# A hybrid attention block on one core: differences of a level in one GpSimd step, norms' halves in tiles of their own, and regrouped matmuls in the output projection

## The chip, the core and the metric

The kernel runs on one core of a Trainium2 chip. A core has TensorE (PE in the profile, with its weight loads as PEld), VectorE (DVE), ScalarE (ACT), GpSimd (POOL) and SyncE (SP, which here only issues DMAs). Each works through its own instructions in a fixed order and waits at semaphores for the others. The metric is the time of one execution on the device in microseconds (us).

## What is computed

One layer of a diffusion backbone, with 256 latent and 256 context tokens of width 2048, all in float32. Its core, cut to what the change touches:

```python
def gla_scan(q, k, v, log_a, s0):            # gated linear attention, 8 heads, forward and backward
    def step(state, inp):
        qc, kc, vc, ac = inp
        b = jnp.cumsum(ac, axis=2)
        o_inter = jnp.einsum('bhid,bhde->bhie', qc * jnp.exp(b), state)
        rel = b[:, :, :, None, :] - b[:, :, None, :, :]
        decay = jnp.exp(jnp.where(lower, rel, -jnp.inf))
        scores = jnp.einsum('bhid,bhjd,bhijd->bhij', qc, kc, decay)
        ...

def hybrid_layer(...):
    h_l = modulate(rms_norm(x, norm1_w), sh1, sc1)
    ... = jnp.split(h_l @ w_in, IN_OFFSETS, axis=-1)        # the same for the context tokens
    ...                                                    # GLA heads: gla_scan both ways
    q_l = rope_2d(diff_qk(dq_l, diff_qnorm_w), ang_row, ang_col)   # rms_norm of each half head
    k_l = rope_2d(diff_qk(dk_l, diff_knorm_w), ang_row, ang_col)
    ...                                                    # differential attention: 8 heads
    g_a, g_b = jnp.split(jax.nn.sigmoid(h @ w_gate + b_gate), 2, axis=-1)
    mix_l = (g_a * (ya @ w_proj_gla) + g_b * (yb @ w_proj_diff)) @ w_out
    x_new = x + g1 * mix_l
    ...                                                    # second norm, conv_ffn, residual
```

## The kernel before

**Precision and weights.** A float32 matrix product is made of products of halves: `split` (L207) copies a weight tile on ACT into `whi` (L212) and subtracts on DVE into `wlo` (L219); both lie in rings of three buffers (tags `hi` and `lo`), each 128x1024. `split_act` (L236) does the same with activations into tiles that its caller gives (L237 on ACT, L238 on DVE). `col_tile` (L255) then makes, for each of 16 weight blocks, one matmul over 512 columns with `whi` (L281, "h") and one over 256 with `wlo` (L283, "l"). `col_tile2` makes three of 512 columns per block (L356 to L358), `value_rows` three of 272 or 512 (L294 to L296).

**Order of the h and l matmuls.** In every run of four blocks the order is `TURN` (h0 l0 h1 l1 h2 l2 h3 l3), or, where `orders` (L249) says so, `SHIFTED` (h0 h1 l0 h2 l1 h3 l2 l3) in two of every seven runs. The output projection, tile `mix`, has 16 output tiles c; it asks for `orders(c, KT // 4, 1, 5)`, so c = 1 to 5 have such runs and c = 6 to 15 have `TURN` alone.

**Stages.** After a first norm and a sweep over the first weights (to about 125 us) come the GLA stage, with the values (`gvb`), queries and keys (`gq`, `gk`), the keys of the other attention (`dk`) and the output gates (`gr`) as matmuls that keep PE busy; then the differential attention (`dvb`, `dq`, the scores `s`) among the `gate` tiles; the two projections (`pga`, `pgb`), `mix`, and the feed-forward part (`upg`, `upv`, `down`), which the change leaves alone.

**A pair of GLA heads.** `gla_pair` (L799) runs four times, with priority over the matmuls around it. Two matmuls (`z`, L812) give the log decays of both directions; four ACT steps each (L816 to L819) and one DVE step (L820) make `m`; DVE scans (L824 to L833) make the cumulative sums `bfb` (forward in row 0, backward in row 1). The scores within 128 tokens are then made at seven levels of halving, m = 64 to 1. For one level `factors` (L899) takes four differences on GpSimd into `e` (L916 to L919: queries and keys, first and second half of every block, each 128x128), one exponential on ACT (L920) and one product with q and k on DVE (L921). `e` has a ring of four buffers. `scored` (L871) runs the score matmuls `sc` (L882) of a group of levels and puts them into `at`: two copies per head on ACT (L932, L933), masked copies on DVE (L929). Groups are: two products that need no level, with levels 0 and 1; levels 2 to 4; levels 5 and 6. Between the first two groups PE transposes the keys (`kT`, L857), which ACT copies to `kn` (L858).

**Norms of the attention's queries and keys.** `heads_norm` (L659) copies a finished `dk` or `dq` tile out of its bank on ACT, squares it into `nsq`, splits the squares with `split`, so through the rings of the weights, sums them with two matmuls (`hss`, L656 and L657), and finishes with ACT and DVE (L318 to L332).

**What sets the order.** No list is written out by hand for this part. The scheduler of the Tile layer orders each engine's instructions with its own estimates of durations and priorities, so an edit in one place moves instructions in others.

**VectorE's side job.** Between these steps DVE runs dot products `araw` over 128x1024 (L380) for the modulation vectors.

Of the kernel before, what the change touches and what calls it, by code (L numbers as in the profile page):

```python
# [9 lines left out]
F32 = mybir.dt.float32  # L10
# [142 lines left out]
def layer_kernel(tc, I, out):  # L153
# [3 lines left out]
    with es:  # L157
# [5 lines left out]
        def acc_bank(name):  # L163
            return ps.tile([P, 512], F32, tag="acc", bufs=4, name=name)
# [481 lines left out]
        gr = [p2.tile([P, 2 * T + 4], F32, tag=f"gr{p}", name=f"gr{p}")[:, :2 * T] for p in range(NPAIR)]  # L646
        dk = [p2.tile([P, 2 * T + 4], F32, tag=f"dk{h}", name=f"dk{h}")[:, :2 * T] for h in range(HEADS)]

        def norm_tiles():
            return [tp.tile([P, 512], F32, tag=t, name=t) for t in ("nraw", "nsq", "hny")]  # L650

        def sums(o, m, sq, halves):

# [2 lines left out]
            i = PE.matmul(o, m, lo[:, :n], start=True, stop=False)  # L656
            after(PE.matmul(o, m, hi[:, :n], start=False, stop=True), i)  # L657

        def heads_norm(b, wname, done, o, sq, y):  # L659
# [24 lines left out]
        def onormed(pool, dst, ob, w, halves=None, copy=V.tensor_copy, places=None):  # L684


            raw, sq, y = places or [pool.tile([P, T], F32, tag=t, name=t) for t in ("oraw", "osq", "ony")]
            S.activation(sq, ob[:, :T], AF.Square)
            copy(raw, ob[:, :T])
            s = aux_bank("oss")  # L690
            if halves is None:
                PE.matmul(s[:, :T], ones.bitcast(F32), sq, start=True, stop=True)
            else:
                split_act(*halves, sq)
                sums(s[:, :T], ones, sq, halves)
            rsqrt_parts(y, sq, s[:, :T], DV)
            normed_by(dst, raw, w, y, sq, DV)

        SHUF = [(j + 16) % 32 for j in range(32)]

# [36 lines left out]
        with tc.tile_pool(name="gla", bufs=1) as pg:  # L737
# [60 lines left out]

            def gla_pair(p):  # L799
                q, kl, kc = qk[p][:, 0, :], qk[p][:, 1, :], qk[p][:, 2, :]  # L800
                bfb = pg.tile([P, 2, T], F32, tag="bfb", name="bfb")
                rc = pg.tile([P, 2, T], F32, tag="rc", name="rc")
                raw = st.tile([P, 1024], F32, tag="raw", bufs=4, name="wr")
                wr = raw[:96, :2 * P].rearrange("p (a b) -> p a b", a=2)
# [93 lines left out]

                def factors(li):  # L899

                    e = pg.tile([P, 2, T], F32, tag="e", bufs=4, name="e")
                    if li is None:
                        S.activation(e[:, 0, P:], bfb[:, 0, P:], AF.Exp, scale=1.0 / 16)
                        S.activation(e[:, 0, :P], bfb[:, 1, :P], AF.Exp, scale=1.0 / 16)
                        S.activation(e[:, 1, :P], bfb[:, 0, :P], AF.Exp, scale=-1.0 / 16, bias=bl[:, 0:1])
                        S.activation(e[:, 1, P:], bfb[:, 1, P:], AF.Exp, scale=-1.0 / 16, bias=bl[:, 1:2])
                    else:
                        m = LEVELS[li]
                        g = T // (2 * m)
                        f4 = bfb[:, 0, :].rearrange("p (g h m) -> p g h m", h=2, m=m)  # L910
                        b4 = bfb[:, 1, :].rearrange("p (g h m) -> p g h m", h=2, m=m)
                        q4 = e[:, 0, :].rearrange("p (g h m) -> p g h m", h=2, m=m)
                        k4 = e[:, 1, :].rearrange("p (g h m) -> p g h m", h=2, m=m)
                        fm = f4[:, :, 0, m - 1:m].to_broadcast([P, g, m])
                        bm = b4[:, :, 1, 0:1].to_broadcast([P, g, m])
                        G.tensor_tensor(q4[:, :, 1, :], f4[:, :, 1, :], fm, op=ALU.subtract)  # L916
                        G.tensor_tensor(q4[:, :, 0, :], b4[:, :, 0, :], bm, op=ALU.subtract)
                        G.tensor_tensor(k4[:, :, 0, :], fm, f4[:, :, 0, :], op=ALU.subtract)
                        G.tensor_tensor(k4[:, :, 1, :], bm, b4[:, :, 1, :], op=ALU.subtract)  # L919
                        S.activation(e, e, AF.Exp, scale=1.0 / 16)  # L920
                    V.tensor_tensor(e, e, qk[p][:, 0:2, :], op=ALU.mult)  # L921
                    return e

# [10 lines left out]
                for n, levels in enumerate(RUNS):  # L934
                    group = ([] if n else whole) + [level(li) for li in levels]
                    if n == 1:
                        sb = scored(group[::-1], states)
                        kept = pg.tile([P, 2, T], F32, tag="e", bufs=4, name="e")
                        state = kept[:, 0, :].rearrange("p (a b) -> p a b", a=2)
                        S.copy(kept[:, 0, :], sb)  # L940
                    else:
                        scored(group[::-1])
                    if n == 0:
                        kn = turned_keys()

                obs = [aux_bank("o", j) for j in range(2)]
                for j in range(2):
# [5 lines left out]
                        PE.matmul(obs[j][:, :T], gv[:, c, h * DV:(h + 1) * DV], at[:, j, c, :],  # L953
                                  start=False, stop=c == 1)
                    if not j:
                        e = pg.tile([P, 2, T], F32, tag="e", bufs=4, name="e")
# [63 lines left out]
        with tc.tile_pool(name="diff", bufs=1) as pd:  # L1020
# [36 lines left out]
            def dq_tile(h):  # L1057
                ada_next(0.5)
                dq[h] = pd.tile([P, T], F32, tag="dq", bufs=4, name="dq")
                b = aux_bank("dq") if h < 2 else acc_bank("dq")  # L1060
                col_tile(I["w_in"][15 - NGK + h], A, b)
                heads_norm(b, nwt[:, 1:2], lambda o: roped(pd, dq[h], o, 1),
                           *[t[:, h % 2 * T:(h % 2 + 1) * T] for t in nts])

            qs, ks = {}, {}

# [34 lines left out]
            def attend(h, c):  # L1101
# [15 lines left out]
                o = pd.tile([P, T], F32, tag="ob", name="ob")  # L1117
                osq = pd.tile([P, 2, T], F32R, tag="osqs", name="osqs")
                onormed(pd, o, ob, nwt[:, 3:4], [osq[:, j, :] for j in range(2)])
# [13 lines left out]
                V.tensor_tensor(gates[j], b[:, T:], gates[j], op=ALU.add)  # L1133

            nts = norm_tiles()
            dv_chunk(0)
            for h in range(4):
                dq_tile(h)
# [298 lines left out]
```

## Time and profile before

| what | value |
|---|---|
| median of three runs | 1673.39 us (1673.18 to 1675.27) |
| the profiled execution: its own time | 1674.66 us |
| its span, first to last instruction | 1672.9 us |
| DVE busy | 1276.8 us, 76% |
| ACT busy | 898.9 us, 54% |
| granted TensorE clock, mean | 0.999 |

The span is 1.8 us shorter than the execution's own time. A row of the profile's groups gives line, engine, operation, tiles (written <- read), shape, count, then busy time and mean duration in ns, then the engine's idle time before these instructions with what ended it. A row of a timeline gives start, duration, engine and the same names, with the idle time before it in square brackets.

### The profile page before, as it was taken

Reading aid. Unit: us, or ns where it says so; the run is one execution under the profiler, and the core shown is the slowest. Engines: PE = TensorE matmul, PEld = TensorE weight load, DVE = VectorE, ACT = ScalarE, POOL = GpSimd, SP = SyncE. Lnnn points to the kernel's source line nnn. Section 1 sums busy time; section 2 is a strip of 40 time slices with the busy share of each in tenths; the row PEclk is TensorE's granted clock in tenths of the full one; section 3 lists DMA queues with packets and bytes.
Section 4 is the critical chain, followed back from the end, with each engine's and each line's share of the span. In section 5 each row is a group of like instructions: output and inputs, shape, how many; then the busy total and the mean of one; then the engine's idle time right before and its main releaser. Section 6 shows DMA issues by size and latency. Waiting matters only on the chain.

```text
span 1672.9 us, 25641 instructions
## 1 busy us (share of the span) xinstructions
PE 1655.4 (99%) x9476; PEld 1408.7 (84%) x9476; DVE 1276.8 (76%) x2013; ACT 898.9 (54%) x1475; POOL 338.0 (20%) x412
## 2 busy tenths in 40 slices
PE   9999999999999999999999999999999999999998
PEld 6679888788878888888888998888888888888887
DVE  5887877768677888788888796888888888744544
ACT  5234455654356776556655575555555555433332
POOL 0011332415011000001214101221222122584000
PEclk9999999999999999999999999999999999999999
DMA  9996735336565555797877566777777776676664
GB/s 383 408 363 216 231 129 167 114 115 207 195 222 179 189 187 194 229 288 261 275 269 233 177 204 211 237 230 229 239 240 238 220 237 214 208 221 208 219 191 137
DMA packets 111965, 372.74 MB, mean 223 GB/s; under 512 B 14560, under 2 KB 19680, under 8 KB 111840
## 3 DMA queue, kind: packets, MB, share of 16 engines
q1 hardware_dynamic: 102112, 362.51, 66.1%
q0 software_dynamic: 5696, 4.24, 1.0%
q10 hardware_dynamic: 4032, 4.37, 0.8%
q8 instruction: 74, 1.21, 0.3%
q14 instruction: 51, 0.42, 0.1%
HBM read 364.73 MB, written 2.10 MB: 219 GB/s over the span
## 4 chain that ended last, share of the span: by engine, by line
PE 91%; DVE 3%; DMA 2%; ACT 1%; POOL 1%; issue 1%; DVEq 0%; SPq 0%; ACTq 0%
PE down L1388 14%; PE upg L281 9%; PE upv L281 9%; PE gate L281 7%; PE upv L283 5%; PE upg L283 5%; PE sweep L392 4%; PE gate L283 4%; PE mix L281 4%; PE mix L283 2%; PE dvb L294 2%; PE pga L281 2%; PE pgb L281 2%; PE dvb L296 2%; PE dvb L295 2%; PE dq L281 1%
## 5 line engine op out<-in xcount | busy, mean ns | idle before, releaser
L212 ACT CAST whi<-wraw 128x1024 fp32r<-128x1024 f32 (+3 forms) x502 | 515.0, 1028 | 427.3 <-PE down L1388 138.6
L219 DVE TENSOR_TENSOR wlo<-wraw,whi 128x1024 fp32r<-128x1024 f32 (+3 forms) x466 | 562.1, 1207 | 208.4 <-ACT whi L212 203.8
L281 PE MATMUL upg<-x,whi 128*128 128x512 f32 x656 | 229.0, 391 | 0.0
L281 PE MATMUL upv<-x,whi 128*128 128x512 f32 x656 | 229.0, 391 | 0.0
L1388 PE MATMUL down<-whi,g 128*128 128x512 f32 x704 | 216.6, 389 | 0.0
L283 PE MATMUL upv<-x,wlo 128*128 128x256 f32 x656 | 182.8, 280 | 0.0
L283 PE MATMUL upg<-x,wlo 128*128 128x256 f32 x656 | 182.6, 280 | 0.0
L281 PE MATMUL gate<-x,whi 128*128 128x512 f32 x512 | 179.2, 397 | 0.0
L380 DVE CUSTOM_DVE_ANT_0 araw<-araw,cb 128x1024 f32<-128x1024 f32 x128 | 161.2, 1263 | 15.1 <-DMA araw<-in_w_ada 15.1
L219 POOL TENSOR_TENSOR wlo<-wraw,whi 128x1024 fp32r<-128x1024 f32 x36 | 87.0, 2416 | 395.4 <-ACT whi L212 395.4
L1388 PEld LDWEIGHTS down<-whi,g 128*128 128x128 f32 x704 | 132.1, 188 | 27.4
L281 PEld LDWEIGHTS upv<-x,whi 128*128 128x128 f32 x656 | 122.4, 187 | 26.6
L281 PEld LDWEIGHTS upg<-x,whi 128*128 128x128 f32 x656 | 122.4, 187 | 26.6
L283 PE MATMUL gate<-x,wlo 128*128 128x256 f32 x512 | 140.7, 284 | 0.2 <-DVE wlo L219 0.2
L1388 PE MATMUL down<-wlo,g 128*128 128x512 f32 x352 | 136.9, 389 | 0.0
L1306 DVE SCALAR_TENSOR_TENSOR C<-C,vec 128x255 f32<-128x255 f32 x88 | 105.7, 1203 | 36.6 <-ACT C L1305 36.6
L283 PEld LDWEIGHTS upg<-x,wlo 128*128 128x128 f32 x656 | 123.9, 189 | 0.5
L283 PEld LDWEIGHTS upv<-x,wlo 128*128 128x128 f32 x656 | 123.9, 189 | 0.5
L281 PEld LDWEIGHTS gate<-x,whi 128*128 128x128 f32 x512 | 94.3, 188 | 19.8 <-issue 0.7
L283 PEld LDWEIGHTS gate<-x,wlo 128*128 128x128 f32 x512 | 96.3, 189 | 5.4 <-issue 2.6
L281 PE MATMUL mix<-x,whi 128*128 128x512 f32 x256 | 88.9, 395 | 0.0
L1388 PEld LDWEIGHTS down<-wlo,g 128*128 128x128 f32 x352 | 66.1, 188 | 13.7
(332 smaller groups left out, 3235.9 us busy)
## 6 DMA issues: line engine op xcount, KB each, us to landing
wraw<-in_w_up SPq DMA_DIRECT2D x164, 512.0 KB, 4.6
araw<-in_w_ada SPq DMA_DIRECT2D x128, 512.0 KB, 5.5
wraw<-in_w_down SPq DMA_DIRECT2D x88, 512.0 KB, 4.4
wraw<-in_w_gate SPq DMA_DIRECT2D x64, 512.0 KB, 4.6
wraw<-in_w_in SPq DMA_DIRECT2D x58, 512.0 KB, 4.8
ada<-in_w_ad SPq DMA_DIRECT2D x52, 512.0 KB, 9.9
wraw<-in_w_proj SPq DMA_DIRECT2D x32, 512.0 KB, 4.9
wraw<-in_w_out SPq DMA_DIRECT2D x32, 512.0 KB, 4.7
```

What stands on the lines that cost most here:

```text
L212: copied[0] = S.copy(hi[:, :n], raw)
L219: i = e.tensor_tensor(lo[:, :n], raw, hi[:, :n].bitcast(F32), op=ALU.subtract)
L281: i = PE.matmul(b.rearrange("p (a b) -> p a b", a=2), whi[:, sl], acts[k], start=first, stop=last)
L283: i = PE.matmul(b[:, T:], wlo[:, sl], acts[k][:, 1, :], start=False, stop=last)
L294: PE.matmul(o, hi[k][:, ts], whi[:, sl], start=first, stop=False)
L295: PE.matmul(o, lo[k][:, ts], whi[:, sl], start=False, stop=False)
L296: return PE.matmul(o, hi[k][:, ts], wlo[:, sl], start=False, stop=last)
L380: i = V.tensor_tensor_reduce(raw, raw, cb[:, q * 1024:(q + 1) * 1024], 1.0, 0.0, op0=ALU.mult, op1=ALU.add, accum_out=ada2[:, j, q:q + 1])
L392: return kept(PE.matmul(*args, **kw))
L1306: V.scalar_tensor_tensor(u[:, 1:], b[:, :T - 1], vcol("conv_w", ct), u[:, 1:], op0=ALU.mult, op1=ALU.add)
L1388: i = PE.matmul(banks[h][t][n], g[:, a, ts], w[n][b], start=k == 0 and (a, b) == (1, 0), stop=k == FT - 1 and b == 1)
```

## The change

Three things are edited.

1. **Differences of a level.** GpSimd makes one subtraction per level, 128x512, into a new tile `away`: all of `bfb` minus the value at the middle of each block (for the backward row one place further, which a row length of T + 1 in the view `shifted` gives). ACT then takes two exponentials of 256 columns: with scale +1/16 for the queries and -1/16 for the keys, each reading the half blocks of the two rows crosswise. `away` has the tag `m`, one buffer, that `m` of the decays has too. The ring of `e` goes from four buffers to three.
2. **Norms.** `heads_norm` splits its squares with `split_act` into a tile `nlo` (and, for 512 columns, into a second that shares the buffer of `hny`), and takes its result tile later. In `onormed` the result may stay in `oraw`, and the shuffled tile `rt` of the queries comes from the other pool.
3. **Output projection.** `orders(c, KT // 4, 1, 14)`: two of seven runs in c = 1 to 14 are `SHIFTED`.

```diff
@@ norms
         def norm_tiles():
-            return [tp.tile([P, 512], F32, tag=t, name=t) for t in ("nraw", "nsq", "hny")]
+            return [tp.tile([P, 512], F32, tag=t, name=t) for t in ("nraw", "nsq")] + [lambda: tp.tile([P, 512], F32, tag="hny", name="hny")]
...
             def parts():
-                halves = split(sq, n)
+                low = tp.tile([P, 512], F32R, tag="nlo", name="nlo")
+                halves = [low[:, j * T:(j + 1) * T] for j in range(2)]
+                if n > T:
+                    halves = tp.tile([P, 512], F32R, tag="hny", name="nhi"), low
+                split_act(*halves, sq)

                 def rest():
+                    y = new()
                     s = acc_bank("hss")
...
@@ gla_pair
-                bfb = pg.tile([P, 2, T], F32, tag="bfb", name="bfb")
+                flat = pg.tile([P, 2 * T + 2], F32, tag="bfb", name="bfb")
+                bfb = flat[:, :2 * T].rearrange("p (a b) -> p a b", a=2)
+                shifted = flat.rearrange("p (a b) -> p a b", a=2)
...
-                    e = pg.tile([P, 2, T], F32, tag="e", bufs=4, name="e")
+                    e = pg.tile([P, 2, T], F32, tag="e", bufs=3, name="e")
...
-                        G.tensor_tensor(q4[:, :, 1, :], f4[:, :, 1, :], fm, op=ALU.subtract)
-                        G.tensor_tensor(q4[:, :, 0, :], b4[:, :, 0, :], bm, op=ALU.subtract)
-                        G.tensor_tensor(k4[:, :, 0, :], fm, f4[:, :, 0, :], op=ALU.subtract)
-                        G.tensor_tensor(k4[:, :, 1, :], bm, b4[:, :, 1, :], op=ALU.subtract)
-                        S.activation(e, e, AF.Exp, scale=1.0 / 16)
+                        away = pg.tile([P, 512], F32, tag="m", name="away")
+                        mids = shifted[:, :, m - 1:T:2 * m].unsqueeze(3).to_broadcast([P, 2, g, 2 * m])
+                        G.tensor_tensor(away.rearrange("p (a g n) -> p a g n", a=2, g=g),
+                                        bfb.rearrange("p a (g n) -> p a g n", g=g), mids, op=ALU.subtract)
+                        for i, (first, step, o, back, sign) in enumerate(((m, T - m, m, -m, 1), (0, T + m, 0, m, -1))):
+                            S.activation(view(e[:, i, :], o, [back, 2], [2 * m, g], [1, m]),
+                                         view(away, first, [step, 2], [2 * m, g], [1, m]), AF.Exp, scale=sign / 16)
...
@@ output projection
-            col_tile(I["w_out"][c], A, b, orders(c, KT // 4, 1, 5) if c else None)
+            col_tile(I["w_out"][c], A, b, orders(c, KT // 4, 1, 14) if c else None)
```

The number of matmuls stays the same; GpSimd has 84 instructions fewer, ACT 28 more. From the output projection on, all orders are as before but for the `mix` matmuls; ahead of it the scheduler has placed much anew. Three places matter below.

ACT where the first `dq` tile is finished (norm of the queries), before:

```order
L212 CAST whi<-wraw 128x1024
L290 COPY nraw<-dq 128x256
L665 ACTIVATE nsq<-nraw 128x256
L212 CAST whi<-nsq 128x256
L212 CAST whi<-wraw 128x1024 x2
L318 ACTIVATE hny<-hss,epsb 128x256
```

The same place in the change:

```order
L212 CAST whi<-wraw 128x1024
L290 COPY nraw<-dq 128x256
L212 CAST whi<-wraw 128x1024
L669 ACTIVATE nsq<-nraw 128x256
L237 CAST nlo<-nsq 128x256
L212 CAST whi<-wraw 128x1024
```

A cast of weights now stands ahead of the squares, and the cast of the squares no longer takes a buffer of the weights' ring.

DVE in the first pair of GLA heads, from the query's scaling to the products of the first levels (`rc` and `qe` are the decayed keys and queries), before:

```order
L763 SCALAR_TENSOR_TENSOR qk<-gq,qk 128x256
L219 TENSOR_TENSOR wlo<-wraw,whi 128x544
L380 ISA araw,ada_77<-araw,cb 128x1024
L380 ISA ada_77 128x1
L837 TENSOR_TENSOR rc<-rc,qk 128x512
L846 TENSOR_TENSOR qe<-qe,qk 128x512
L921 TENSOR_TENSOR e<-e,qk 128x512 x4
```

The same place in the change:

```order
L774 SCALAR_TENSOR_TENSOR qk<-gq,qk 128x256
L219 TENSOR_TENSOR wlo<-wraw,whi 128x544
L380 ISA araw,ada_77<-araw,cb 128x1024
L380 ISA ada_77 128x1
L850 TENSOR_TENSOR rc<-rc,qk 128x512
L859 TENSOR_TENSOR qe<-qe,qk 128x512
L930 TENSOR_TENSOR e<-e,qk 128x512 x2
L219 TENSOR_TENSOR wlo<-wraw,whi 128x544
L380 ISA araw,ada_77<-araw,cb 128x1024
L380 ISA ada_77 128x1
L930 TENSOR_TENSOR e<-e,qk 128x512
```

The third product, the last that the first group of scores needs, now stands behind a weight split and a dot product. On PE, in the same pair, 16 more `gvb` matmuls stand ahead of these scores.

ACT between the decays of the first pair (`z`) and the bank that the next query tile needs (`gvb`), before:

```order
L816 ACTIVATE m<-z,nba 128x512
L817 ACTIVATE l<-z,vec 128x512
L818 ACTIVATE l<-l 128x512
L819 ACTIVATE l<-l 128x512
L212 CAST whi<-wraw 128x1024
L749 COPY gv<-gvb 128x272
```

The same place in the change:

```order
L829 ACTIVATE m<-z,nba 128x512
L830 ACTIVATE l<-z,vec 128x512
L212 CAST whi<-wraw 128x1024
L831 ACTIVATE l<-l 128x512
L832 ACTIVATE l<-l 128x512
L212 CAST whi<-wraw 128x1024
L760 COPY gv<-gvb 128x272
```

Before, the first of the two 128x1024 casts stood ahead of these six rows; it now stands behind the two steps that read `z`.

More of the change, by code (lines that the diff above doesn't have):

```diff
@@ L657, in sums, with heads_norm @@
             after(PE.matmul(o, m, hi[:, :n], start=False, stop=True), i)
-        def heads_norm(b, wname, done, o, sq, y):
+        def heads_norm(b, wname, done, o, sq, new):
             n = o.shape[1]
@@ L937, in gla_pair @@
                         sb = scored(group[::-1], states)
-                        kept = pg.tile([P, 2, T], F32, tag="e", bufs=4, name="e")
+                        kept = pg.tile([P, 2, T], F32, tag="e", bufs=3, name="e")
                         state = kept[:, 0, :].rearrange("p (a b) -> p a b", a=2)
@@ L955, in gla_pair @@
                     if not j:
-                        e = pg.tile([P, 2, T], F32, tag="e", bufs=4, name="e")
+                        e = pg.tile([P, 2, T], F32, tag="e", bufs=3, name="e")
                     places = e[:, 0, :], e[:, 1, :], kept[:, 1, :]
@@ L1061, in dq_tile @@
                 col_tile(I["w_in"][15 - NGK + h], A, b)
[L1062 to L1063 removed]
+                heads_norm(b, nwt[:, 1:2], lambda o: roped(tp, dq[h], o),
+                           *[t[:, h % 2 * T:(h % 2 + 1) * T] for t in nts[:2]], lambda: nts[2][:, h % 2 * T:(h % 2 + 1) * T])
             qs, ks = {}, {}
@@ L1116, in attend @@
                     PE.matmul(ob[:, :T], dv[:, t, h * DV:(h + 1) * DV], pTs[h][:, t, :], start=t == 0, stop=t == 3)
-                o = pd.tile([P, T], F32, tag="ob", name="ob")
                 osq = pd.tile([P, 2, T], F32R, tag="osqs", name="osqs")
-                onormed(pd, o, ob, nwt[:, 3:4], [osq[:, j, :] for j in range(2)])
+                o = onormed(pd, None, ob, nwt[:, 3:4], [osq[:, j, :] for j in range(2)])
                 yb[h] = p2.tile([P, 2 * T + 4], F32R, tag=f"dk{h}", name=f"yb{h}")[:, :2 * T]
@@ L1135, in layer_kernel @@
             nts = norm_tiles()
+            nts[2] = nts[2]()
             dv_chunk(0)
```

11 lines of the change are left out of this document (5 added, 6 removed).

## The prediction

> **What bounds the kernel now.** I read the page first (busy shares), then PE's waits, then the busy time in stretches, and last the timelines around the waits.
>
> ```profile
> span 1672.9 us, 25641 instructions
> PE 1655.4 (99%) x9476; PEld 1408.7 (84%) x9476; DVE 1276.8 (76%) x2013; ACT 898.9 (54%) x1475; POOL 338.0 (20%) x412
> ```
>
> TensorE works for 99% of the span. A change that leaves its matmuls alone can win only where PE stands idle, or where its matmuls follow each other a little closer. GpSimd is busy for a fifth of the time, so 84 fewer instructions there are worth nothing by themselves. What they are worth is read from PE's waits:
>
> ```profile
> PE sc L882 <- DVE e L921: 1.9, 2, 1.6
> PE gr L281 <- ACT whi L212: 1.3, 1, 1.3
> PE gq L281 <- ACT gv L749: 1.0, 1, 1.0
> PE dq L281 <- ACT whi L212: 1.0, 2, 0.6
> PE kT L857 <- ACT at L933: 1.0, 1, 1.0
> PE dvb L294 <- ACT whi L212: 0.8, 1, 0.8
> PE sc L882 <- ACT kn L858: 0.7, 1, 0.7
> PE gr L283 <- DVE wlo L219: 0.5, 1, 0.5
> PE hss L656 <- DVE wlo L219: 0.2, 1, 0.2
> ```
>
> Columns are the total in us, the number of waits, the longest. All nine rows lie in the GLA stage and the start of the next one, and they add up to 8.4 us. That is the whole prize, 0.5% of the time; what is left of PE's idle time lies at the very start and end of the program, which the change doesn't touch. In the GLA stage idle is not the rule either:
>
> ```profile
> 160.00:200.00 40.00, 37.59 (x316) 35.55 (x314) 35.77 (x64) 22.52 (x46) 20.69 (x28) 1.00 0.67 204
> 1600.00:1640.00 40.00, 40.00 (x178) 33.14 (x177) 18.06 (x15) 15.75 (x15) 0.00 (x0) 1.00 0.63 192
> 156.00:161.90 5.90, 5.90 (x48) 5.74 (x46) 2.61 (x4) 3.66 (x6) 0.00 (x0) 1.00 0.88 315
> ```
>
> These are stretches of the span with busy time and count of PE, PEld, DVE, ACT and POOL. In the first, the first pair of heads, PE lacks 2.4 us while DVE is busy for 35.8 of 40: DVE is the crowded engine beside PE. The second gives the pace of 512-column matmuls, 40/178 = 0.225 us, the third that of the `gvb` matmuls, 5.90/48 = 0.123 us.
>
> **The change part by part. GpSimd's step.**
>
> ```profile
> L917 POOL TENSOR_TENSOR e<-bfb 128x128 f32<-128x128 f32 x28 | 22.3, 796 | 6.0 <-DVE bfb L831 6.0
> L918 POOL TENSOR_TENSOR e<-bfb 128x128 f32<-128x128 f32 x28 | 21.6, 772 | 0.0
> L916 POOL TENSOR_TENSOR e<-bfb 128x128 f32<-128x128 f32 x28 | 20.7, 739 | 117.3 <-DVE bfb L824 99.2 <-PE sc L882 12.2 <-DVE ada L380 4.4
> L919 POOL TENSOR_TENSOR e<-bfb 128x128 f32<-128x128 f32 x28 | 19.0, 677 | 0.0
> 251.15 1.41 POOL L917 TENSOR_TENSOR e<-bfb 128x128 f32<-128x128 f32 x1
> 252.52 0.40 POOL L918 TENSOR_TENSOR e<-bfb 128x128 f32<-128x128 f32 x1
> 143.82 0.74 POOL L705 TENSOR_TENSOR dk<-nraw,rope 128x256 f32<-128x256 f32 x1 [16.96 <-DVE nraw L332]
> 1205.22 2.42 POOL L219 TENSOR_TENSOR wlo<-wraw,whi 128x1024 fp32r<-128x1024 f32 x1 [8.69 <-ACT whi L212]
> ```
>
> Four steps of a level take 0.80 + 0.77 + 0.74 + 0.68 = 2.98 us on average. Undisturbed, one takes 0.40; some take 1.41. One step of 128x512 is not in the trace. Between the rows of 256 (0.74) and 1024 elements (2.42) it comes to 0.74 + 256 x 1.68/768 = 1.3 us; the two rows are its bounds, and I take 1.3 alone and up to 2.3 when it is held up once, by the 1.0 us between 1.41 and 0.40. ACT pays for it:
>
> ```profile
> L920 ACT ACTIVATE e<-e 128x512 f32<-128x512 f32 x28 | 17.6, 631 | 27.3 <-POOL e L919 27.2
> L321 ACT ACTIVATE e<-e 128x256 f32<-128x256 f32 x7 | 3.0, 425 | 0.1
> ```
>
> Two steps of 256 cost 0.85 in place of 0.63, 28 times 0.22, so 6 us more on an engine that is half idle: hidden, except where a cast for PE stands behind. On the level's own path it is 1.3 to 2.3 plus 0.85, so 2.2 to 3.2 us, against 3.0 + 0.6. But before, GpSimd began the next level while ACT worked on this one, so a level came every 3.0 us. Now `away` has one buffer, and GpSimd waits for ACT's second exponential. A level comes every 2.2 to 3.2 us, and behind a weight cast later still. **The chain of levels becomes hardly faster**; what changes is where its waits fall in PE's order. The smaller ring of `e` adds nothing within a group of three levels; across groups ACT, no longer GpSimd, waits for the score matmuls.
>
> **First pair of heads.**
>
> ```profile
> 184.27 0.44 PE L857 MATMUL kT<-ident,rc 128*128 128x128 f32 x2 [1.00 <-ACT at L933]
> 175.86 2.69 DVE L921 TENSOR_TENSOR e<-e,qk 128x512 f32<-128x512 f32 x4
> 178.47 0.71 DVE L219 TENSOR_TENSOR wlo<-wraw,whi 128x544 fp32r<-128x544 f32 x1
> L380 DVE CUSTOM_DVE_ANT_0 araw<-araw,cb 128x1024 f32<-128x1024 f32 x128 | 161.2, 1263 | 15.1 <-DMA araw<-in_w_ada 15.1
> ```
>
> Of the waits listed, 1.3 us lie here: 1.00 for `kT`, and the 0.3 by which the two waits of `sc` for `e` exceed their longest, which is the third pair's. Now the third product stands behind one more split (0.71) and one more dot product (1.26): 2.0 us later. PE has 16 more `gvb` matmuls ahead of it: 16 x 0.123 = 2.0 us. That evens out; the decays are ready about 1.2 us earlier (below), and GpSimd's longer steps hold DVE up once or twice by up to 1.3 us. In the second group `kT` still waits for copies on ACT that now stand behind both exponentials of level 3. Ends: all 1.3 gone, or 3 more; I take **0.8 us worse**, as both counted delays stand ahead of the product.
>
> **Bank of the next query tile.**
>
> ```profile
> 158.18 1.05 ACT L212 CAST whi<-wraw 128x1024 fp32r<-128x1024 f32 x1 [4.85 <-DVE ada L380]
> 162.56 0.38 ACT L749 COPY gv<-gvb 128x272 f32<-128x272 f32 x1
> 162.99 0.50 PE L281 MATMUL gq<-x,whi 128*128 128x512 f32 x1 [1.03 <-ACT gv L749]
> ```
>
> ACT idled 4.85 us ahead of the cast at 158.18. In the new order the two steps that read `z` use that time; the cast, two steps of 512 columns (0.63, as `L920` above), the second cast and the copy then end at about 158.2 + 1.05 + 1.26 + 1.05 + 0.38 = 161.9, and PE wants the bank at 162.99 - 1.03 = 161.96. Of 1.0 us I leave 0.2: **0.8 better** (0 to 1.0).
>
> **Third pair.** Its waits are 1.6 (the longest of `sc` for `e`) and 0.7 (`kn`). Between the pair's second `z` and its first scores PE's order had 48 `dk` and 32 `gr` matmuls, now 64 and 32: 16 x 0.225 = 3.6 us more. DVE's third product has a `nlo` (0.67, as a product of 512, 2.69/4), a split of 1024 and a dot product newly ahead of it, about 3.2 us, of which about 0.9 goes back as a shuffle and a sum of the keys now stand earlier. So the product comes some 2.3 us later, 3.3 with a hold-up, against 3.6 of cover: the 1.6 falls to 0.3 to 1.3. I take 0.6 left of the 2.3 together: **1.7 better** (2.3 to -1). Pairs two and four have no wait now; in the new order 17 to 24 us of matmuls lie between second `z` and scores, about what the chain took in the first pair, so I add **0.3** for a wait there (0 to 2).
>
> **Norms' halves.**
>
> ```profile
> 452.22 0.41 ACT L212 CAST whi<-nsq 128x256 fp32r<-128x256 f32 x1
> 452.53 2.12 ACT L212 CAST whi<-wraw 128x1024 fp32r<-128x1024 f32 x2
> 454.70 0.50 PE L281 MATMUL dq<-x,whi 128*128 128x512 f32 x1 [0.55 <-ACT whi L212]
> ```
>
> ACT cast the squares first, then two weight tiles, and PE waited 0.55 us for the second; three such waits make the rows `dq` (1.0) and `dvb` (0.8). In the new order one cast of weights stands ahead of the squares, and the ring of three is free of them. The second cast comes earlier by at least the square's own 0.41 and its cast's 0.41, more than 0.55. I take 0.4 left of 1.8: **1.4 better** (0 to 1.8). At the `dk` tiles the waits are `gr` 1.3 and 0.5 and `hss` 0.2. There the squares meet a `z` and an output norm on ACT, and these stay; only the ring is freed. I take half and a little: **1.1 better** of 2.0 (-0.5 to 2.0).
>
> **Output projection.**
>
> ```profile
> 875.89:881.46 5.57, 5.57 (x34) 4.88 (x33) 0.95 (x2) 1.00 0.87 291
> 892.57:898.11 5.54, 5.54 (x34) 4.88 (x33) 0.96 (x2) 1.00 0.52 140
> 915.20:920.85 5.65, 5.65 (x34) 4.89 (x33) 0.97 (x2) 1.00 0.64 204
> ```
>
> These stretches run from first matmul to first matmul: tile c = 5 (with regrouped runs), 8 and 12 (without). `TURN` runs at two paces, 5.54 and, in c = 11 to 14, 5.65; the regrouped ones at 5.57. Four tiles lose 0.03, four gain 0.08: **0.2 better** (0.1 worse to 0.4 better).
>
> **Sum.** +0.8 - 0.8 - 1.7 + 0.3 - 1.4 - 1.1 - 0.2 = -4.1 us. The profiled execution would take 1674.66 - 4.1 = 1670.6, with a span of 1668.8. The median of three runs, 1673.39, lies 1.3 below the profiled time, so the forecast is 1669.3.
>
> **A rule that speaks against it.** In one place the trace shows DVE and GpSimd excluding each other:
>
> ```profile
> 1201.82 0.48 DVE L1306 SCALAR_TENSOR_TENSOR C<-C,vec 128x255 f32<-128x255 f32 x1
> 1205.62 2.30 DVE L1306 SCALAR_TENSOR_TENSOR C<-C,vec 128x255 f32<-128x255 f32 x1 [0.99 <-ACT C L1305]
> ```
>
> The same DVE step takes 0.48 alone and 2.30 when it starts 0.4 us into GpSimd's step of 2.42. The Trainium skill, SBUF — State Buffer, section "Who interferes with whom", says that a DVE instruction with two SBUF inputs and a GpSimd instruction that reads SBUF exclude each other for the whole instruction, whichever was issued first. By that rule, with which these rows agree, one step of 1.3 us blocks DVE longer at a time than four short ones with gaps; the first rival prices it.
>
> **The rivals.** (1) *Slower: the long step blocks DVE at the wrong moment.* A hold-up of 1.3 us in front of the product or split that PE needs next moves a whole group of scores; eight groups (first and second of four pairs) are exposed. Gains outside the levels are 0.8 + 1.4 + 1.1 + 0.2 = 3.5, so from three groups on (3.9) the kernel is slower. With six, 7.8 - 3.5 = 4.3 worse: 1677.7. For it: DVE's 89% in the first stretch. Against: four short steps were held up too, to 1.41. Chance 0.15. (2) *The idle time only moves.* The scheduler places scores where its own estimate has them ready; where that is wrong by as much as before, 8.4 us stand elsewhere: 1673.2. Chance 0.15. (3) *The change doesn't do what it says for the norms:* the casts wait for data or for ACT's queue, not for the ring, and 2.5 us stay: 1671.8. For it: ACT's steps around the `dk` norms are as many as before. Chance 0.13. (4) *All idle goes:* 1673.4 - 8.6 = 1664.8. Chance 0.11. The forecast, 1667 to 1671.5, has 0.46.
>
> **How the numbers follow.** A measurement of this kernel can tell about 0.2%, 3.3 us, from no change: faster means under 1670.0, slower over 1676.7. Of the forecast's 0.46 about 0.39 lie under 1670.0; with rival 4 that makes 0.50 faster. The rest of it, 2 and 3 make 0.35 the same; rival 1 makes 0.15 slower. The range 1665.5 to 1676.0 leaves out half of rival 4 and most of rival 1.
>
> **What would show it.** Right: no waits of `dq` and `dvb` for `whi`; `gq` within 0.2 us; `away` at 1.3 to 2.3 us; PE idle in the GLA stage at 4 to 5 us in place of 8.4; tiles c = 11 to 14 at 5.58. Wrong: DVE products at 2 us beside `away`, PE waiting for `e` or `wlo` in pairs two and four, or a sum of PE's waits of 8 us or more.

## The result and the profile after

The changed kernel takes **1669.13 us** (median of seven runs, 1668.38 to 1669.92) against 1674.64 (seven runs, 1673.18 to 1675.27) for the kernel before on the same chip: ratio 0.9968, 95% interval 0.9957 to 0.998. The profiled executions took 1669.92 and 1674.66 us. So 5.5 us are gone by the medians and 4.74 by the profiled executions, where 4.1 were forecast. One execution of `away_two_tiles`, an experiment below, took 3562.12 us and is left out of its median.

The page of the changed kernel, span and busy times:

```profile
span 1668.1 us, 25627 instructions
PE 1652.1 (99%) x9476; PEld 1409.8 (85%) x9476; DVE 1284.1 (77%) x2013; ACT 901.4 (54%) x1503; POOL 298.4 (18%) x328
```

TensorE has the same 9476 matmuls, yet its busy time fell by 3.3 us (1655.4 to 1652.1). DVE's rose by 7.3. PE's waits of the changed kernel behind the first sweep (total, number, longest, in us):

```profile
PE hss L660 <- DVE nlo L238: 2.9, 2, 1.7
PE sc L895 <- DVE at L938: 1.8, 1, 1.8
PE o L962 <- DVE at L938: 1.3, 1, 1.3
...
PE mix L283 <- DVE wlo L219: 0.6, 1, 0.6
...
PE gvb L296 <- DVE wlo L219: 0.3, 1, 0.3
...
PE pga L283 <- DVE wlo L219: 0.2, 1, 0.2
```

None of the nine rows of before is left, nor a tenth, in the attention stage, that the prediction leaves out:

```profile
PE gate L283 <- DVE wlo L219: 0.2, 1, 0.2
```

Three larger rows took their place, all for DVE: the sums of a norm's squares (`hss`) for `nlo`, and in the last pair of heads the scores and the outputs for masked copies `at`. The sum is 7.1 us, against 8.6 before: listed idle alone explains 1.5 of the 4.8 us by which the span fell.

So the better view is the length of a stage between two matmuls that have the same place in the order of both kernels: from the first `gq` to the first `dq` (the GLA stage), from there to the first `pga`, and the output projection from its first matmul to the first `up`. Columns: stretch, its length, then busy time and count of PE, PEld, DVE, ACT and POOL. Before:

```profile
126.08:445.10 319.02, 312.20 (x1890) 266.65 (x1889) 245.00 (x420) 166.53 (x312) 95.92 (x129) 1.00 0.54 173
445.10:758.20 313.10, 311.12 (x1729) 262.45 (x1728) 247.03 (x445) 193.27 (x344) 19.09 (x24) 1.00 0.65 211
848.00:937.80 89.80, 89.77 (x513) 78.19 (x512) 74.13 (x104) 45.61 (x64) 29.15 (x47) 1.00 0.75 245
```

After:

```profile
126.10:441.20 315.10, 310.46 (x1889) 266.84 (x1888) 253.69 (x416) 170.43 (x339) 54.31 (x45) 1.00 0.55 177
441.20:752.80 311.60, 309.93 (x1729) 262.93 (x1728) 244.19 (x447) 192.10 (x346) 20.18 (x24) 1.00 0.66 210
843.10:933.10 90.00, 89.44 (x514) 77.99 (x513) 74.34 (x104) 45.51 (x64) 30.30 (x47) 1.00 0.75 244
```

The GLA stage is 3.9 us shorter, the attention stage 1.5, the output projection 0.2 longer. For the GLA stage one profile is not exact: it took 317.75 us in `only_mix` (below), which has the orders of before there, and 313.99 in a second profile of the changed kernel. The projections between the last two stretches are 0.5 longer (848.0 - 758.2 against 843.1 - 752.8). In the attention stage PE's idle time (length less busy) fell only from 1.98 to 1.67: the other 1.2 us are in the *busy* time of the same 1729 matmuls.

The new step and the product behind it, after:

```profile
L925 POOL TENSOR_TENSOR away<-bfb 128x512 f32<-128x512 f32 x28 | 38.6, 1378 | 120.4 <-ACT e L928 66.2 <-DVE bl L853 41.4 <-DVE rc L846 12.8
L930 DVE TENSOR_TENSOR e<-e,qk 128x512 f32<-128x512 f32 x32 | 25.7, 814 | 2.7 <-ACT e L928 2.7
```

A step takes 1.38 us on average, inside the 1.3 to 2.3 forecast. What ends GpSimd's idle time is new: before, it was the scan of the *first* direction (99.2 of 117.3 us, `bfb` L824); now it is ACT's exponentials (`e` L928) and DVE's steps behind the scans of the *second* (`bl` L853, `rc` L846).

### The profile page after: what moved, and what is told of

Read it like the earlier page. It is cut to its first block, busy times and chain, and to the rows that moved or that the text cites. A ratio compares the mean times of both kernels' runs of the same rounds, so it can differ in the third digit from the quotient of the medians.

```text
span 1668.1 us, 25627 instructions
## 1 busy us (share of the span) xinstructions
PE 1652.1 (99%) x9476; PEld 1409.8 (85%) x9476; DVE 1284.1 (77%) x2013; ACT 901.4 (54%) x1503; POOL 298.4 (18%) x328
## 4 chain that ended last, share of the span: by engine, by line
PE 72%; DVE 1%; DMA 0%; issue 0%; ACT 0%; SPq 0%; DVEq 0%
PE down L1397 14%; PE upg L281 9%; PE upv L281 9%; PE gate L281 7%; PE upv L283 5%; PE upg L283 5%; PE mix L281 4%; PE gate L283 3%; PE mix L283 2%; PE pgb L281 2%; PE pga L281 2%; PE dq L281 2%; PE dvb L295 1%; PE dvb L296 1%; PE dvb L294 1%; PE pga L283 1%
```

## The experiments

**The parts by themselves.** `only_levels` has the new level and no more, `only_norms` the whole second edit with the smaller ring of `e` (the new tile `nlo` takes the memory of the fourth buffer), `only_ring3` that ring alone, `only_mix` the regrouped runs alone, `levels_norms` levels and norms without the regrouping. Against the kernel before, the two smallest edits are:

```diff
# only_ring3, in all three places
-                    e = pg.tile([P, 2, T], F32, tag="e", bufs=4, name="e")
+                    e = pg.tile([P, 2, T], F32, tag="e", bufs=3, name="e")
# only_mix
-            col_tile(I["w_out"][c], A, b, orders(c, KT // 4, 1, 5) if c else None)
+            col_tile(I["w_out"][c], A, b, orders(c, KT // 4, 1, 14) if c else None)
```

> The kernel before with the first edit alone (one GpSimd step per level, crossed exponentials, ring of e at three buffers). Theory A, each edit removes its own waits of TensorE: the wait for the query bank goes (-0.8 us) and the third pair's waits shrink (-1.7), the waits of dq, dvb, gr and hss stay at about 3.8 us; 2 to 3 us faster than before. Theory B, the scheduler only deals the waits out anew: the sum of TensorE's waits stays at 7 to 9 us, and the time within 1.5 us of the kernel before or of the changed one without any relation to the edits.

> The kernel before with the norms' halves in own tiles alone (the ring of e at three buffers, since the new tile takes its place in memory; four GpSimd steps per level as before). Theory A: the waits of dq and dvb for whi (1.8 us) go and those at the keys' norms halve (-1.0); the waits around the first and third pair's scores (1.9 + 1.0 + 0.7) stay; 2 to 3 us faster. A rival to A: the smaller ring of e alone holds GpSimd back and costs 1 us or more, so that less than 1.5 us remain. Theory B: as for the levels alone.

> The changed kernel without the regrouped output projection. Theory A: the changed kernel's time plus 0.2 to 0.4 us, with the same waits in the stages ahead of the output projection, and output tiles 11 to 14 back at 5.65 us each in place of 5.57.

> The kernel before with the regrouped output projection alone. All orders ahead of it are as before, so both theories give the same: 0.1 to 0.4 us faster, which the time can hardly tell; the profile shows it: tiles 6 to 9 at 5.57 us in place of 5.55, tiles 11 to 14 at 5.57 in place of 5.65, TensorE's waits ahead of it as before.

> The kernel before with the ring of e at three buffers and nothing else, which the norms alone had beside them. Theory A (the norms' own tiles carry the gain of that kernel, 7.6 us): within 2 us of the kernel before, or slower, since GpSimd waits longer for a free buffer. Rival (the smaller ring makes the scheduler place the scores better): 3 us or more faster.

| kernel | median, us | before beside it | ratio, 95% interval |
|---|---|---|---|
| `only_levels` | 1681.74 | 1673.81 | 1.0046 [1.0031, 1.0061] |
| `only_norms` | 1666.16 | 1673.81 | 0.995 [0.9933, 0.9966] |
| `levels_norms` | 1668.74 | 1673.81 | 0.9966 [0.9953, 0.9979] |
| `only_mix` | 1674.72 | 1673.81 | 1.0002 [0.9993, 1.0011] |
| `only_ring3` | 1673.69 | 1673.83 | 0.9999 [0.999, 1.0009] |

The norms' own tiles carry more than the whole gain: 7.6 us. The new level costs 7.9 alone and 2.6 beside the norms; ring and regrouping change nothing that can be measured. The first two expectations missed: `only_levels` was to be 2 to 3 us faster, or within 1.5 us of one of the two kernels, and `only_norms` 2 to 3 us faster. PE's waits of `only_norms`:

```profile
PE hss L656 <- DVE nlo L238: 1.7, 1, 1.7
...
PE sc L889 <- DVE rc L828: 1.0, 1, 1.0
PE sc L889 <- DVE e L928: 0.9, 1, 0.9
PE o L960 <- DVE at L936: 0.8, 1, 0.8
```

Besides `dq`, `dvb` and `gr`, the waits of `gq` (1.0) and `kT` (1.0) and those of the third pair (1.6 and 0.7) are gone too, which my sum had put down to the new levels. The wait of `gq` is missing in the profile of `only_mix` as well, so it isn't in every execution of the orders of before. The waits of `only_levels`, the three longest and the two for `whi`:

```profile
PE sc L888 <- DVE e L923: 4.7, 2, 3.3
PE gk L358 <- DVE wlo L219: 1.9, 1, 1.9
PE dq L281 <- DVE e L323: 1.5, 1, 1.5
...
PE dq L281 <- ACT whi L212: 1.0, 2, 0.5
...
PE dvb L294 <- ACT whi L212: 0.7, 1, 0.7
```

Without the norms' tiles the waits of `dq` and `dvb` for `whi` stay, and scores of the third and the fourth pair wait 4.7 us for a product `e`: the opposite of the 1.7 that I had taken off.

**Is it GpSimd's long step?** Three variants of `levels_norms`: the subtraction on DVE, in two GpSimd steps of 256, and with two of a pair's seven levels in the buffer of `l`.

```diff
# away_on_dve
-                        G.tensor_tensor(away.rearrange("p (a g n) -> p a g n", a=2, g=g),
+                        V.tensor_tensor(away.rearrange("p (a g n) -> p a g n", a=2, g=g),
# two_steps
-                        G.tensor_tensor(away.rearrange("p (a g n) -> p a g n", a=2, g=g),
-                                        bfb.rearrange("p a (g n) -> p a g n", g=g), mids, op=ALU.subtract)
+                        for a in range(2):
+                            G.tensor_tensor(away.rearrange("p (a g n) -> p a g n", a=2, g=g)[:, a],
+                                            bfb.rearrange("p a (g n) -> p a g n", g=g)[:, a], mids[:, a], op=ALU.subtract)
# away_two_tiles
-                        away = pg.tile([P, 512], F32, tag="m", name="away")
+                        away = pg.tile([P, 512], F32, tag="l" if li in (1, 5) else "m", name="away")
```

> Levels and norms as changed, the subtraction of a level on VectorE in place of GpSimd (regrouping of the output projection left out, as in all runs with levels and norms below). Theory lock (GpSimd's step of 1.38 us keeps VectorE's two-input steps out for its whole length, which costs VectorE about 11 us over the kernel with norms alone): the subtraction takes about 0.7 us on VectorE and nothing is kept out, so the 28 steps cost 19 us of work but 11 go; VectorE's other steps get back their durations of the kernel with norms alone, and the time stays within 3 us of levels and norms. Theory one buffer (the single tile of the differences makes the levels wait for ScalarE): the waits for scores stay as with GpSimd, and 19 us more work on the crowded engine make it 3 us or more slower.

> Levels and norms, each level's subtraction in two GpSimd steps of 256 elements (0.74 us each) in place of one of 512. Theory lock by length: a hold-up of VectorE falls from 1.3 to 0.7 us at a time; the products of the levels and the splits beside them get shorter on average, TensorE's waits for scores shrink, 1 to 3 us faster than levels and norms. Rival (what counts is GpSimd's whole time per level, not its pieces): the same within 1 us, or slower, since a level may now be held up twice.

> Levels and norms, with the differences of levels 1 and 5 in the buffer of l in place of that of m, so that GpSimd need not wait for ScalarE's exponentials between the two levels of the first and of the last group. Theory one buffer: the first scores of each pair come about 0.8 us earlier; 1 to 3 us faster than levels and norms, with fewer idle us of GpSimd behind ScalarE. Theory lock: no gain beyond 1 us, since GpSimd's steps then follow each other and keep VectorE out for longer in one stretch.

`away_on_dve` took 1671.37 us (ratio 0.9989 [0.9979, 0.9998]), `two_steps` 1668.76 (0.9972 [0.996, 0.9983]), `away_two_tiles` 1670.48 (0.9979 [0.9968, 0.9989]), each beside 1673.83. None comes near the 1666 of the norms alone. Halving the step or taking it off GpSimd doesn't bring the loss back, though the 28 steps on DVE cost time of their own. The one-buffer theory missed its figures too: `away_on_dve` was to be 3 us or more slower than `levels_norms` (1668.74, on another chip) and came 2.6 slower, and `away_two_tiles` was to be 1 to 3 us faster and came 1.7 slower. All three still write into a buffer of the decays, `m` or `l`. In `away_on_dve` and `away_two_tiles` one step also reads both directions, so that with two tiles GpSimd's first step waits for the scan of the second direction (`bfb` L844, 58.7 us in three pairs) whatever buffer is free. In `two_steps` the first half reads the forward direction alone; in the second pair it still waits for DVE's steps behind the second:

```profile
242.75 3.04 POOL L926 TENSOR_TENSOR away<-bfb 128x256 f32<-128x256 f32 x2 [13.73 <-DVE bl L853]
```

**ScalarE's second step, the buffer, and the norms again.** Two variants of `only_norms` take apart what is left of the level: two exponentials in place of one, and in the second kernel the four old GpSimd steps also go through `away`.

```diff
# norms_two_exps
-                        S.activation(e, e, AF.Exp, scale=1.0 / 16)
+                        for i in range(2):
+                            S.activation(e[:, i, :], e[:, i, :], AF.Exp, scale=1.0 / 16)
# norms_away_four
-                        q4 = e[:, 0, :].rearrange("p (g h m) -> p g h m", h=2, m=m)
-                        k4 = e[:, 1, :].rearrange("p (g h m) -> p g h m", h=2, m=m)
+                        away = pg.tile([P, 512], F32, tag="m", name="away").rearrange("p (a b) -> p a b", a=2)
+                        q4 = away[:, 0, :].rearrange("p (g h m) -> p g h m", h=2, m=m)
+                        k4 = away[:, 1, :].rearrange("p (g h m) -> p g h m", h=2, m=m)
...
-                        S.activation(e, e, AF.Exp, scale=1.0 / 16)
+                        for i in range(2):
+                            S.activation(e[:, i, :], away[:, i, :], AF.Exp, scale=1.0 / 16)
```

> The norms' part with the old levels (four GpSimd steps straight into e, ring of e 3), and only the exponential of a level in two ScalarE steps of 256 instead of one of 512. Beside the kernel before, the norms' part alone took 7.6 us off and the norms with the new levels 5.1. Theory A (the new levels cost through GpSimd's long step and VectorE's steps beside it): 28 x 0.22 us on a half idle ScalarE are hidden, 1666 us, VectorE busy for about 1272. Theory B (ScalarE's second step lengthens each level): 1668 to 1669 us, TensorE waits for e or at. Theory C (any other order of the levels loses some us): 1668 to 1670 us without a common wait.

> As the run before, and the four GpSimd steps write into the one buffer away, out of which the two exponentials read. The long GpSimd step is all that is missing from the new levels. Theory A (long step, VectorE beside it): 1666 us, VectorE busy for about 1272, GpSimd for about 330. Theory B (ScalarE's second step) 1668 to 1669, as the run before. Theory D (the single buffer keeps GpSimd from working ahead): 1668 to 1671 us while the run before stays at 1666, GpSimd's waits for ScalarE at its first step.

> The norms' part alone (ring of e 3) once more, beside the whole change on one chip. If it is the better version: 1666 us, 2.5 to 3 us below the whole change; TensorE's waits after the sweep about 4.5 us. If the first result was chance: 1668.5 to 1669.5, as the whole change.

> The whole change once more on the chip of the runs before it: 1669 us, 4.5 to 5.5 us below the kernel before; 2.5 to 3 us above the norms' part alone if that is the better version, within 0.5 of it if not.

| kernel, all on one chip | median, us (range) | ratio to before (1674.08), 95% interval |
|---|---|---|
| `norms_again` | 1665.76 (1665.33 to 1666.16) | 0.9951 [0.9939, 0.9964] |
| `norms_two_exps` | 1666.16 (1665.8 to 1666.94) | 0.9954 [0.9941, 0.9968] |
| `norms_away_four` | 1669.07 (1668.66 to 1669.4) | 0.9971 [0.9959, 0.9982] |
| `full_again` | 1668.77 (1668.27 to 1670.52) | 0.997 [0.9958, 0.9981] |

The second exponential is hidden: its 0.4 us over `norms_again` lies within ranges that overlap. The buffer alone, with four short steps and no long one, costs 2.9 us over `norms_two_exps` and brings the kernel to the time of the whole change. In the profiles 2.4 of the 2.9 lie in the GLA stage; the output projection, which has the same orders in both, takes 89.8 against 89.2 (on its two paces see the next section). The norms' part by itself beats both kernels: no run of it overlaps with one of the whole change.

The timeline of GpSimd shows what the buffer does. Second pair of heads, `norms_again` (start, duration, line and operation, idle time before it and its releaser):

```profile
226.66 0.40 POOL L923 TENSOR_TENSOR e<-bfb 128x128 f32<-128x128 f32 x1 [36.60 <-PE z L819]
227.02 0.40 POOL L925 TENSOR_TENSOR e<-bfb 128x128 f32<-128x128 f32 x1
227.37 1.39 POOL L923 TENSOR_TENSOR e<-bfb 128x128 f32<-128x128 f32 x1
228.73 1.38 POOL L925 TENSOR_TENSOR e<-bfb 128x128 f32<-128x128 f32 x1
...
238.88 0.70 POOL L924 TENSOR_TENSOR e<-bfb 128x128 f32<-128x128 f32 x1 [5.50 <-DVE bfb L838]
```

The same place in `norms_away_four`:

```profile
243.49 1.30 POOL L924 TENSOR_TENSOR away<-bfb 128x128 f32<-128x128 f32 x1 [13.70 <-DVE bl L847]
...
248.28 0.89 POOL L924 TENSOR_TENSOR away<-bfb 128x128 f32<-128x128 f32 x1 [0.53 <-ACT e L929]
```

The first steps of this pair in the kernel before, and the first one in the change:

```profile
233.98 0.61 POOL L916 TENSOR_TENSOR e<-bfb 128x128 f32<-128x128 f32 x1 [42.01 <-DVE bfb L824]
...
242.31 0.70 POOL L917 TENSOR_TENSOR e<-bfb 128x128 f32<-128x128 f32 x1 [0.67 <-DVE bfb L831]
```

```profile
243.28 1.92 POOL L925 TENSOR_TENSOR away<-bfb 128x512 f32<-128x512 f32 x1 [13.73 <-DVE bl L853]
```

With the old buffers GpSimd subtracts the forward halves of two levels at 226.7 to 230.1, while the backward direction is still to come; its last scan stands at 238.4. The kernel before did so for three levels. In `norms_away_four` the same subtraction, which reads the forward half alone, waits until 243.5 for DVE's step behind the last reader of the decays `m` (`rc`, L840, which ends at 243.35), because `away` *is* the buffer of `m`; in the fourth pair the row names `rc` itself. After that the levels come one by one, each waiting for ACT. In the change the work ahead of time is lost twice over: its one step also reads both directions, so it could not start before the last scan ends (at 242.5), even with a buffer of its own. From DVE's last backward scan to the third product that the first scores need, in `norms_again`:

```profile
238.40 0.40 DVE L838 TENSOR_TENSOR_SCAN bfb<-ones,m 128x128 f32<-128x128 f32 x1
...
243.04 1.28 DVE L928 TENSOR_TENSOR e<-e,qk 128x512 f32<-128x512 f32 x2
```

and in `norms_away_four`:

```profile
242.37 0.40 DVE L838 TENSOR_TENSOR_SCAN bfb<-ones,m 128x128 f32<-128x128 f32 x1
242.69 0.66 DVE L840 TENSOR_TENSOR_SCAN rc<-ones,m 128x255 f32<-128x255 f32 x1
...
252.17 0.69 DVE L930 TENSOR_TENSOR e<-e,qk 128x512 f32<-128x512 f32 x1 [1.10 <-ACT e L929]
```

From the scan's end to the third product's end that is 244.32 - 238.80 = 5.5 us against 252.86 - 242.77 = 10.1. Most of the difference is other work that the new order puts in between: two weight splits, a dot product and an `nlo` (4.8 us), where `norms_again` has one split (1.4); DVE idles for 1.1. The stretches from the first `gq` to the first `dq` show where most of the 3 us stands, for `norms_again`, PE busy 310.13 of 312.12:

```profile
126.18:438.30 312.12, 310.13 (x1890) 266.79 (x1889) 240.84 (x411) 166.13 (x309) 85.59 (x129) 1.00 0.55 178
```

and for `norms_away_four`, 310.38 of 315.00:

```profile
126.20:441.20 315.00, 310.38 (x1890) 266.68 (x1889) 244.90 (x411) 170.11 (x337) 100.74 (x129) 1.00 0.53 177
```

PE idles 4.6 us in place of 2.0, and the changed kernel has the same 4.6 (315.10 less 310.46). PE does not wait for scores in the second pair in either kernel: they stand at 247.0 us in `norms_again` and at 254.6 in `norms_away_four`. Most of the idle time stands in the fourth pair, for a product and for masked copies of its second and third group; in `norms_again`:

```profile
406.24 1.68 PE L889 MATMUL sc<-e 64*128 64x128 f32 x24 [1.28 <-DVE e L928]
...
428.74 1.99 PE L960 MATMUL o<-at,gv 128*128 128x256 f32 x8 [0.25 <-DVE at L936]
```

and in `norms_away_four`:

```profile
408.84 0.71 PE L889 MATMUL sc<-e 64*128 64x128 f32 x8 [2.54 <-DVE e L930]
...
431.82 0.48 PE L962 MATMUL o<-at,gv 128*128 128x256 f32 x1 [1.50 <-DVE at L938]
```

The separation holds in every profile: the GLA stage takes 312.1 to 312.9 us in the three that have the norms' tiles and no `away`, and 314.0 to 316.2 in the seven that have both.

**What stays open.** In the kernels with `away` in `m` the second pair's first `z` also stands later in PE's order (224.7 us against 219.8). How much of the 3 us is that new order, and how much the wait inside a pair, was not separated. A buffer of its own for `away`, with four steps, was not run; one step over both directions would wait for the second one there too. `away_two_tiles` places its decays early (216.0 us) and still gains nothing; beyond the wait for the second scan its cause was not followed further.

## Why the prediction was right, and where its steps were not

The time was right (1669.13 for 1669.3), and so was the attention stage (1.5 us gained for 1.4); in the GLA stage the terms add up to 2.5 and it gained 3.9. The causes were not right. By the edits:

| edit | forecast | measured |
|---|---|---|
| new levels (first pair +0.8, bank of `gq` -0.8, third pair -1.7, pairs two and four +0.3) | -1.4 | +2.6 beside the norms, +7.9 alone |
| norms' tiles (at `dq` and `dvb` -1.4, at `dk` -1.1) | -2.5 | -7.6, and -8.3 in the second run |
| output projection | -0.2 | no change in time; in the profile's stage +0.2 over before, +0.8 over `levels_norms` |

- **First pair, bank of `gq`, third pair.** All these waits did go: `kT` 1.0, `gq` 1.0, and the third pair's 1.6 and 0.7. But the norms alone remove them, and the wait of `gq` comes and goes with the orders of before. The failed step is giving a reordering that the diff makes as a whole to one of its edits.
- **The chain of levels becomes hardly faster.** This is the step that failed. I saw that `away` has one buffer and that GpSimd would wait for ACT, but counted a level's period only. That GpSimd worked ahead between the two directions stood in the row `L916`: 99.2 of its 117.3 us of idle time ended by the *first* direction's scan. I didn't ask what ends it when one step reads both directions and its destination is the decays' own buffer. In the second pair the chain behind the last scan went from 5.5 to 10.1 us between `norms_again` and `norms_away_four`, and the new levels cost 2.6 us where I had 1.4 gained.
- **Pairs two and four.** I put 0.3 here (0 to 2). The second pair has no wait; the fourth has two, of 1.8 and 1.3 us, 3.1 in all. The place was right for one pair of two, and the size was a tenth of what came.
- **Norms.** That the edit removes the waits for `whi` is right: no `dq` or `dvb` has one. Whether the freed ring does it, or the new places of other tiles in the same edit, was not separated. Rival 3 (1671.8) falls. Of the 2.0 us at the `dk` tiles 1.2 are left, as a wait of `hss` for `nlo` (none with the norms alone). The term was too small by 5.1 us because I counted these waits alone, and the edit reorders the whole GLA stage: that took 312.9 us in `only_norms`, against 319.0 before. Why this order is so much better stays open. A new wait of 1.67 us for `nlo` stands in the attention stage, so its listed idle hardly fell; the stage still became 1.5 us shorter, about what I had forecast, but mostly in busy time (last section).
- **Output projection.** Tiles c = 11 to 14 did come to 5.57 us, as forecast. But tiles with `TURN` have two paces there: 5.65 in the profiles of before, `only_ring3`, `away_on_dve` and `norms_away_four`, and 5.55 in all others with this order, `levels_norms` among them, which was expected back at 5.65. The whole stage, in `norms_again` and in `norms_away_four`:

```profile
839.70:928.90 89.20, 89.18 (x513) 78.11 (x512) 74.73 (x104) 45.59 (x64) 28.91 (x47) 1.00 0.75 246
842.60:932.40 89.80, 89.77 (x514) 78.25 (x513) 74.11 (x104) 45.61 (x64) 29.16 (x47) 1.00 0.74 245
```

  I had taken the slower pace for a property of the order. What sets it is not shown. The regrouped stage (90.0 us in three profiles) adds a wait of 0.6 us for `wlo` and gains nothing: it is 0.2 us longer than the slow pace and 0.8 than the fast one.
- **Rival 1, the long step.** DVE does become slower beside it: its product takes 0.81 us on average in the changed kernel, 0.72 in the norms alone, and its busy time rises from 1273.1 to 1284.2 between `norms_again` and `full_again`. With the subtraction moved to DVE (`away_on_dve`, 28 steps of 0.68 us) its busy time is 1281.6, against 1283.6 in `levels_norms`: the rest of its work takes 21 us less. Products of 2 us, the sign that I had named, did not come; the longest took 1.58. With four short steps (`norms_away_four`) DVE is busy for 1276.5 us and the kernel is as slow: the lengthening costs no time that can be measured. The Trainium skill, SBUF — State Buffer, section "Who interferes with whom", says that a DVE instruction with two SBUF inputs contends with a GpSimd instruction that reads SBUF; the longer DVE steps agree with it, but what it would make of the time did not come.
- **Rivals 2 and 4.** Listed idle did mostly move, as rival 2 has it: 7.1 of 8.6 us stand elsewhere. Its time of 1673.2 did not come, since PE's busy time fell as well. It didn't all go either. The 4 to 5 us that I had named for the GLA stage fit its stretch (4.6), but the stretch had 6.8 before, not 8.4.

The forecast held because an underestimated gain (5.1 us too small) and a missed loss (4.0) nearly cancelled. That is luck.

## What to carry to other kernels

When an edit merges steps or gives a step a new destination, ask which of its inputs comes last, whose buffer it writes and when that buffer's last reader is done. The row that names the releaser of the producer's idle time shows what it did ahead of time; a step that needs the last input, or a shared buffer, takes that away. Test the parts of a change alone, also when the whole is a gain: here one part beats the whole by 3.0 us (1665.76 against 1668.77). And measure stages between matmuls of equal place, not by the sum of idle rows, and in more than one profile: the GLA stage of the changed kernel differed by 1.1 us between two (315.10 and 313.99).

## What the runs showed of the hardware that I had not expected

**A wait is partly shown as work.** PE's busy time fell by 3.3 us with the same matmuls. In the timeline of the changed kernel, a matmul after a wait and those behind it:

```profile
902.57 0.39 PE L283 MATMUL mix<-x,wlo 128*128 128x256 f32 x1 [0.56 <-DVE wlo L219]
902.80 0.39 PE L281 MATMUL mix<-x,whi 128*128 128x512 f32 x1
903.03 0.28 PE L283 MATMUL mix<-x,wlo 128*128 128x256 f32 x1
```

The 512-column matmul is drawn 0.39 us long, but the next one starts 0.23 after it, so a matmul that comes up to 0.16 us late leaves no idle time in the records. And the 256-column matmul right behind the wait is drawn 0.39 us long, where the same form takes 0.28 two rows on. In the attention stage such hidden time can be traced to one place, the sums of the squares. Two of these matmuls before, and two in the change:

```profile
562.22 0.47 PE L656 MATMUL hss<-wlo,bones 128*128 128x256 f32 x1
562.53 0.28 PE L657 MATMUL hss<-whi,bones 128*128 128x256 f32 x1
```

```profile
585.77 0.28 PE L660 MATMUL hss<-nlo,bones 128*128 128x256 f32 x1
585.89 0.29 PE L661 MATMUL hss<-nlo,bones 128*128 128x256 f32 x1
```

From each start to the next matmul's start, the 16 `hss` of this stage take 3.24 us before and 2.17 in the change; of the 1.07 only 0.22 stood as idle time. What the rest of the 3.3 us is was not shown.

**The parts do not add up.** Levels alone +7.9, norms alone -7.6, regrouping +0.9 at most: the sum would be about the time of before or slower, the whole is 5.5 us faster. The levels cost three times as much where the norms' squares still went through the weights' ring.
